# First loads in the order of use and the first projection in halves of its rows, in a two-layer transformer trunk on one core

## The chip, the core and the metric

The kernel runs on one core of a Trainium2 chip. TensorE (PE in the rows, PEld for its weight loads) multiplies, VectorE (DVE) and ScalarE (ACT) do the elementwise work, GpSimd (POOL) makes constants, SyncE (SP) issues the transfers between HBM and the core's memory; 16 DMA engines carry them. The metric is the device time of one execution in microseconds (us). Three runs of the kernel before gave 1373.3 to 1374.16 us, median 1373.78 us.

## The reference, cut to what matters

Two layers, 256 rows of x, width 1024. Each layer begins with one wide projection of x, and this first projection of the first layer is where the change lies:

```python
def hybrid_mixer(x, cos, sin, w_in, ...):
    proj = x @ w_in                                   # (256, 1024) @ (1024, 6664)
    u, qkv_dil, qkv_fox, f_logit, g_logit = jnp.split(proj, offsets, axis=-1)
    y_ssm = s5_mixer(u, ...)
    qd, kd, vd = ...                                  # from qkv_dil
    qd = partial_rotary(qd, cos, sin) * scale         # cos, sin from positions
    qf, kf, vf = ...                                  # from qkv_fox
    ...
```

Then come the three mixer branches, cross-attention into a memory, and a feed-forward part (dense in layer 0, eight experts in layer 1), each followed by a layer norm.

## The kernel before

Every f32 product is made of three passes of TensorE: the high parts of both factors, then high by low, then low by high (`mm3`). The weights come in pieces of 1 MB (`raw`), taken from a list, `plan`, in the order in which they are used. `split` cuts half a piece (128 x 1024) into its parts: ScalarE copies the high part, VectorE subtracts it for the low part. x must lie with its features along the partitions: `half_features` transposes four 128 x 128 blocks on TensorE, and `parts` writes the high part (`xth`, ScalarE) and the low part (`xtl`, VectorE). `x_features(0)` does that for rows 0 to 127, `x_features(1)` for rows 128 to 255.

`load_x` issues the first loads: two halves of the rows 0 to 127, the first piece of weights, two halves of the rows 128 to 255, the second piece. The first projection makes `vv` (256 x 512) from these two pieces in `gemm_xs`. Its argument `mid` is x's second half: the products of the first 128 rows are made with both pieces (24 products of 128 x 512 columns), then `mid` is called, then the 24 products of the other 128 rows follow; those with their splits are kept in `held`.

Beside this, generators (`side`) hand out small work, one piece at each `tick`: the constants (`make_constants`, at its end `rope_tables`, which loads the positions and makes the sines of the rotary embedding) and the parameters of the state space branch (`ssm_params`). The order of the instructions on each engine is made by a scheduler when the program is built, from the order of the code and its own durations; each engine then works in that order, and an instruction that waits holds all that stand behind it on that engine. `issue_after` binds an instruction in that order behind another. Loads are issued by SyncE's queue; eight semaphores take turns, so a load waits for the landing of the eighth before it.

Of the kernel before, what the change touches and what calls it, by code (L numbers as in the profile page):

```python
# [1 line left out]

# [5 lines left out]
F32 = mybir.dt.float32  # L8
F32R = mybir.dt.float32r
I32 = mybir.dt.int32  # L10
# [6 lines left out]
P = 128  # L17
D = 1024
KT = 8
S = 256  # L20
NT = 2
# [27 lines left out]
HALVES = (slice(0, 512), slice(512, 1024))  # L49


class Trunk:
# [5 lines left out]
    def __init__(self, tc, a, out):  # L58
        self.tc, self.nc, self.a, self.out = tc, tc.nc, a, out
        self.depth = 2  # L60
        self.on_pool = 0
        self.plan, self.issued, self.pos, self.raw = [], 0, 0, {}
        self.sides, self.later = [], []

# [148 lines left out]
    def split(self, raw, keep=False):  # L215

        k, n = raw.shape[1], raw.shape[2]
        if keep:
            t = self.slot([P, 2, k, n], F32R, name="split")
        else:  # L220
            t = self.splits.tile([P, 2, k, n], F32R, name="split", tag="split")
        self.nc.scalar.copy(t[:, 0], raw)  # L222
        if self.on_pool > 0:

            self.on_pool -= 1
            for i in range(2):
                self.nc.gpsimd.tensor_sub(t[:, 1, i], raw[:, i], t[:, 0, i].bitcast(F32))
        else:
            self.nc.vector.tensor_sub(t[:, 1], raw, t[:, 0].bitcast(F32))  # L229
        return t[:, 0], t[:, 1]  # L230

    def parts(self, dst, ps, scale=1.0):

        self.nc.scalar.mul(dst[0], ps, scale)  # L234
        hi = dst[0].bitcast(F32)
        if scale == 1.0:
            self.nc.vector.tensor_sub(dst[1], ps, hi)  # L237
        else:
            self.nc.vector.scalar_tensor_tensor(dst[1], ps, scale, hi, op0=ALU.mult, op1=ALU.subtract)

    def mm3(self, ps, left, right, first, last):
        (lh, ll), (rh, rl) = left, right
        mm = self.nc.tensor.matmul
        mm(ps, lh, rh, start=first, stop=False)  # L244
        mm(ps, lh, rl, start=False, stop=False)  # L245
        mm(ps, ll, rh, start=False, stop=last)  # L246

    def gemm_ws(self, chunks, k, mov, evac):

# [18 lines left out]
                        pair += 1  # L268
                self.tick()

    def gemm_xs(self, groups, stat, evac, mid=None, kt=KT):

        for g in range(groups):
            ps, held = None, []
            for half in range(kt // 4):
                raw = self.next_raw()
                n = raw.shape[2]
                if ps is None:  # L280
                    ps = [self.bank(self.mm)[:, :n] for _ in range(NT)]

                def one(t, k, parts):
                    for j in range(2):
                        s = slice(t * P, t * P + P)
                        self.mm3(ps[t], (stat[0][:, k + j, s], stat[1][:, k + j, s]),
                                 (parts[0][:, j], parts[1][:, j]), k + j == 0, k + j == kt - 1)

                for c in range(0, 4, 2):
                    parts = self.split(raw[:, c:c + 2])  # L290
                    k = half * 4 + c
                    if mid:
                        held.append((k, parts))
                        one(0, k, parts)
                    else:
                        for t in range(NT):
                            one(t, k, parts)
                        self.tick()
            evac(g, 0, ps[0])
            if mid:  # L300
                mid()
            for k, parts in held:
                one(1, k, parts)
                self.tick()
            evac(g, 1, ps[1])

    def banks4(self, name):
# [127 lines left out]
    def rope_tables(self):  # L435
        import numpy as np

        nc, c = self.nc, self.const
        pos = c.tile([P, NT], I32, name="pos")
        nc.sync.dma_start(pos, self.a["positions"].rearrange("o (t p) -> p (o t)", p=P),  # L440
                          allow_slow_non_contiguous=True)
        posf = c.tile([P, NT], F32, name="posf")
        nc.vector.tensor_copy(posf, pos)
        inv = np.float32(ROPE_THETA) ** (-np.arange(0, 16, 2, dtype=np.float32) / np.float32(16))
        freq = c.tile([P, ROPE_HALF], F32, name="freq")
        for j in range(ROPE_HALF):
            nc.gpsimd.memset(freq[:, j:j + 1], float(inv[j]))
        ang = c.tile([P, NT, ROPE_HALF], F32, name="ang")
        for t in range(NT):
            nc.vector.tensor_scalar_mul(ang[:, t], freq, posf[:, t:t + 1])  # L450
        self.rcos = c.tile([P, NT, ROPE_HALF], F32, name="rcos")
        self.rsin = c.tile([P, NT, ROPE_HALF], F32, name="rsin")
        w = c.tile([P, NT, ROPE_HALF], F32, name="rw")
        self.sincos(ang, self.rsin, self.rcos, w)
        nc.vector.tensor_scalar_add(self.rcos, self.rcos, 1.0)
# [21 lines left out]
        return (self.slot([P, KT, S], F32R, name=name + "h"), self.slot([P, KT, S], F32R, name=name + "l"))  # L477

    def load_x(self):
        self.x = self.slot([P, NT, D], name="x")  # L480
        src = self.a["x"].rearrange("o (t p) d -> p (o t) d", p=P)
        for t in range(NT):
            for h in range(2):
                s = slice(h * 512, h * 512 + 512)
                self.nc.sync.dma_start(self.x[:, t, s], src[:, t, s])
            self.prefetch(t + 1)

    def load_gb(self, g, b):
        gb = self.slot([P, 2, D], name="gb")
# [41 lines left out]
    def ssm_params(self):  # L531

        nc, c, a = self.nc, self.const, self.a
        n = DEPTH * NPIECE
        rows = self.work([n, 3, P], "lamrows")
        nc.sync.dma_start(rows[:, 0], a["ssm_lambda_re"].rearrange("l (i g) s -> (l i) (g s)", g=2))
        nc.sync.dma_start(rows[:, 1], a["ssm_lambda_im"].rearrange("l (i g) s -> (l i) (g s)", g=2))
        ldt = self.sm([n, 2], "ldt", bufs=1)
        nc.sync.dma_start(ldt, a["ssm_log_dt"].rearrange("l (i g) -> (l i) g", g=2))
        drow = self.work([DEPTH * 4, P], "drow")  # L540
        nc.sync.dma_start(drow, a["ssm_d"].rearrange("l (k p) -> (l k) p", p=P))
        nc.vector.tensor_copy(rows[:, 2].rearrange("p (g s) -> p g s", g=2),
                              ldt[:, :, None].to_broadcast([n, 2, 64]))
        yield
        ps = self.bank(self.aux, "lam")
        for j in range(3):
            nc.tensor.transpose(ps[:, j * n:(j + 1) * n], rows[:, j], self.ident[:n, :n])
        nc.tensor.transpose(ps[:, 3 * n:3 * n + 8], drow, self.ident[:8, :8])
        lam = self.work([P, 16, n], "lamw")
        nc.vector.tensor_copy(lam[:, 0:3].rearrange("p a b -> p (a b)"), ps[:, :3 * n])  # L550
        self.dskip = c.tile([P, DEPTH * 4], F32, name="dskip")
# [1 line left out]
        lre, lim, dt, are, ang, sn, cm, w, th, e1, e2, den, t1, t2, nr, ni = (lam[:, j] for j in range(16))  # L553
# [412 lines left out]
    def mixer(self, l):  # L966
        nc = self.nc

        def ssm_all():
            if l == 0:  # L970
                yield from self.ssm_params()
                yield from self.ssm_layer_params(0)
            yield from self.ssm_steps(l)
# [2 lines left out]
        vv = self.slot([P, 2, NT, BW], name="vv")  # L976
        if l == 0:
            ssm = self.side(ssm_all(), .4)
        self.gemm_xs(1, self.xt, lambda g, t, ps: nc.scalar.copy(vv[:, 0, t], ps),
                     mid=lambda: self.x_features(1))  # L980
        if l == 0:
            self.load_mem()
            for t in range(NT):
# [59 lines left out]
        w, gp = self.gelu, self.gelup  # L1043
# [18 lines left out]
        ps = self.gemm_down(KT, lambda k, t: tuple(m[:, k, t * P:t * P + P] for m in mp))  # L1062
# [396 lines left out]
```

## Time and profile before

| | |
|---|---|
| median of three runs | 1373.78 us |
| the profiled execution | 1373.86 us |
| its span, first to last instruction | 1372.1 us |
| TensorE busy in the span | 1342.3 us, 98% |
| VectorE busy | 1075.0 us, 78% |
| ScalarE busy | 814.4 us, 59% |
| last product of the first projection starts | 23.99 us |

TensorE is busy nearly throughout, so a time is lost or won where it stands idle or runs slowly. The list of instructions in order of time gives each one's start, duration, engine, line of the kernel, operation and operands, and in brackets how long the engine stood idle before it and for whom. A busy TensorE is modelled: the distance from one product's start to the next is the better measure of its pace.

### The profile page before, as it was taken

What the parts mean: (1) busy time and instruction counts of PE and PEld (TensorE: products, weight loads), DVE (VectorE), ACT (ScalarE), POOL (GpSimd) and SP (SyncE); (2) the same over time, 40 slices, a digit from 0 to 9 for tenths busy, and PEclk for the clock granted to TensorE, in tenths of its full rate; (3) what the DMA queues carried; (4) which work ended last, traced back from release to release, by engine and by line L of the source; (5) the groups of instructions that cost most, each with busy time, mean ns of one, the idle gap of its engine ahead of it and who ended that gap; (6) DMA issues with size and microseconds to landing.
All of it is one profiled execution on the core that took longest, in us unless ns stands there. A gap on an engine that the chain in (4) does not pass through costs nothing. (4 is left out here: it accounts for less than half of the span.)

```text
span 1372.1 us, 20754 instructions
## 1 busy us (share of the span) xinstructions
PE 1342.3 (98%) x8086; PEld 1163.5 (85%) x8086; DVE 1075.0 (78%) x1721; ACT 814.4 (59%) x1186; POOL 39.1 (3%) x65
## 2 busy tenths in 40 slices
PE   7999999999999999999999999998999999999995
PEld 6997778889899999889777888987888888888884
DVE  6898779687675696567779668758989889888987
ACT  5658654554454644444766454543877777877873
POOL 1000000000000000010000000014000000000000
PEclk9999999999999999999999999997999999999998
DMA  9452457744672347634235764462999999999980
GB/s 308 125 185 71 145 185 254 268 142 165 214 232 92 123 138 253 224 111 151 93 123 199 274 227 133 171 255 74 354 357 323 355 343 330 359 337 335 345 321 32
DMA packets 175114, 299.37 MB, mean 218 GB/s; under 512 B 19288, under 2 KB 88992, under 8 KB 175008
## 3 DMA queue, kind: packets, MB, share of 16 engines
q1 hardware_dynamic: 175008, 297.97, 62.7%
q8 instruction: 65, 1.06, 0.3%
q14 instruction: 41, 0.34, 0.1%
HBM read 295.85 MB, written 1.05 MB: 216 GB/s over the span
## 5 line engine op out<-in xcount | busy, mean ns | idle before, releaser
L229 DVE TENSOR_TENSOR split<-raw,split 128x1024 fp32r<-128x1024 f32 (+1 forms) x555 | 648.5, 1191 | 196.0 <-ACT split L222 189.7
L222 ACT CAST split<-raw 128x1024 fp32r<-128x1024 f32 (+1 forms) x558 | 564.1, 1027 | 319.3 <-PE bank L246 121.1
L244 PE MATMUL bank<-xth,split 128*128 128x256 f32 x672 | 191.2, 285 | 0.0
L245 PE MATMUL bank<-xtl,split 128*128 128x256 f32 x672 | 190.3, 283 | 0.0
L246 PE MATMUL bank<-xth,split 128*128 128x256 f32 x672 | 190.2, 283 | 0.0
L244 PE MATMUL gu<-split,xgh 128*128 128x512 f32 (+1 forms) x384 | 144.4, 376 | 0.0
L245 PE MATMUL gu<-split,xgh 128*128 128x512 f32 (+1 forms) x384 | 143.0, 372 | 0.1
L246 PE MATMUL gu<-split,xgl 128*128 128x512 f32 (+1 forms) x384 | 142.7, 372 | 0.0
L244 PE MATMUL bank<-split,xth 128*128 128x512 f32 x320 | 130.0, 406 | 4.6 <-ACT xth L234 4.6
L244 PEld LDWEIGHTS bank<-xth,split 128*128 128x128 f32 x672 | 128.9, 192 | 0.6 <-issue 0.2
L245 PEld LDWEIGHTS bank<-xtl,split 128*128 128x128 f32 x672 | 128.9, 192 | 0.4
L246 PEld LDWEIGHTS bank<-xth,split 128*128 128x128 f32 x672 | 128.9, 192 | 0.1
L246 PE MATMUL bank<-split,xtl 128*128 128x512 f32 x320 | 125.8, 394 | 0.3 <-DVE xtl L237 0.3
L245 PE MATMUL bank<-split,xth 128*128 128x512 f32 x320 | 125.7, 393 | 0.0
L245 PEld LDWEIGHTS gu<-split,xgh 128*128 128x128 f32 x384 | 72.2, 188 | 11.3 <-DVE split L229 1.4
L246 PEld LDWEIGHTS gu<-split,xgl 128*128 128x128 f32 x384 | 72.1, 188 | 10.2
L244 PEld LDWEIGHTS gu<-split,xgh 128*128 128x128 f32 x384 | 72.2, 188 | 10.0
L244 PEld LDWEIGHTS bank<-split,xth 128*128 128x128 f32 x320 | 60.5, 189 | 19.8 <-ACT xth L234 5.5
L246 PEld LDWEIGHTS bank<-split,xtl 128*128 128x128 f32 x320 | 60.5, 189 | 14.3 <-DVE xtl L237 0.9
L245 PEld LDWEIGHTS bank<-split,xth 128*128 128x128 f32 x320 | 60.7, 190 | 11.3 <-DVE split L229 0.2
L245 PE MATMUL yd<-split,hth 128*128 128x512 f32 x176 | 69.1, 393 | 0.0
L246 PE MATMUL yd<-split,htl 128*128 128x512 f32 x176 | 68.8, 391 | 0.0
(420 smaller groups left out, 2336.1 us busy)
## 6 DMA issues: line engine op xcount, KB each, us to landing
raw<-in_w_in_dram SPq DMA_DIRECT2D x52, 1024.0 KB, 5.3
raw<-in_moe_w_down_dram SPq DMA_DIRECT2D x40, 1024.0 KB, 6.7
raw<-in_moe_w_gate_dram SPq DMA_DIRECT2D x32, 1024.0 KB, 7.4
raw<-in_moe_w_up_dram SPq DMA_DIRECT2D x32, 1024.0 KB, 7.3
raw<-in_w_branch_dram SPq DMA_DIRECT2D x12, 1024.0 KB, 5.0
raw<-in_moe_w_gate_dram SPq DMA_DIRECT2D x16, 768.0 KB, 7.1
raw<-in_moe_w_up_dram SPq DMA_DIRECT2D x16, 768.0 KB, 6.5
raw<-in_ffn_w_gate_dram SPq DMA_DIRECT2D x11, 1024.0 KB, 5.3
```

The source lines that it names most:

```text
L222: self.nc.scalar.copy(t[:, 0], raw)
L229: self.nc.vector.tensor_sub(t[:, 1], raw, t[:, 0].bitcast(F32))
L244: mm(ps, lh, rh, start=first, stop=False)
L245: mm(ps, lh, rl, start=False, stop=False)
L246: mm(ps, ll, rh, start=False, stop=last)
```

## The change

The loads: `load_x` issues the first piece of weights in two transfers of half its size, and the positions, which `rope_tables` loaded late, directly behind x's second half and ahead of the second piece of weights. The positions are 256 single numbers of 4 bytes, one for each row of x, put on 128 partitions.

The order: `queued` binds the splits of the first projection on ScalarE behind x's features. The first projection runs in halves of its rows only over the first piece: 12 products of the rows 0 to 127, `mid`, 12 products of the rows 128 to 255, and then the second piece for all rows (`late=False`). The eight transposes of `mid` are bound behind the product before them. In `ssm_params` two `yield` are added, and a copy and the transposes are bound behind a split and a product.

```diff
@@ split, queued, parts, mm3
-        self.nc.scalar.copy(t[:, 0], raw)
+        with self.queued():
+            self.nc.scalar.copy(t[:, 0], raw)
...
-            self.nc.vector.tensor_sub(t[:, 1], raw, t[:, 0].bitcast(F32))
+            self.rest = self.nc.vector.tensor_sub(t[:, 1], raw, t[:, 0].bitcast(F32))
...
+    @contextlib.contextmanager
+    def queued(self):
+        with contextlib.ExitStack() as stack:
+            for i in self.ahead:
+                stack.enter_context(self.tc.issue_after(i.ins))
+            yield
...
-        self.nc.scalar.mul(dst[0], ps, scale)
+        self.featured = self.nc.scalar.mul(dst[0], ps, scale)
...
-        mm(ps, ll, rh, start=False, stop=last)
+        self.product = mm(ps, ll, rh, start=False, stop=last)
@@ gemm_xs
+                def second():
+                    with self.tc.issue_after(self.product.ins):
+                        mid()
+                    if self.ahead:
+                        self.ahead = [self.featured]
+                    for k, parts in held:
+                        one(1, k, parts)
+                        self.tick()
+
                 for c in range(0, 4, 2):
                     parts = self.split(raw[:, c:c + 2])
                     k = half * 4 + c
-                    if mid:
+                    if mid and (late or half == 0):
                         held.append((k, parts))
                         one(0, k, parts)
                     else:
                         for t in range(NT):
                             one(t, k, parts)
                         self.tick()
+                if mid and not late and half == 0:
+                    second()
             evac(g, 0, ps[0])
-            if mid:
-                mid()
-            for k, parts in held:
-                one(1, k, parts)
-                self.tick()
+            if mid and late:
+                second()
             evac(g, 1, ps[1])
@@ rope_tables
-        pos = c.tile([P, NT], I32, name="pos")
-        nc.sync.dma_start(pos, self.a["positions"].rearrange("o (t p) -> p (o t)", p=P),
-                          allow_slow_non_contiguous=True)
         posf = c.tile([P, NT], F32, name="posf")
-        nc.vector.tensor_copy(posf, pos)
+        nc.vector.tensor_copy(posf, self.positions)
@@ load_x
         for t in range(NT):
-            for h in range(2):
-                s = slice(h * 512, h * 512 + 512)
+            for s in HALVES:
                 self.nc.sync.dma_start(self.x[:, t, s], src[:, t, s])
-            self.prefetch(t + 1)
+            if t == 0:
+                w, k, n = self.plan[0]
+                self.raw[0] = raw = self.slot([P, k, n], name="raw")
+                for j in range(0, k, 2):
+                    self.nc.sync.dma_start(raw[:, j:j + 2], w[:, j:j + 2])
+                self.issued = 1
+        self.positions = self.const.tile([P, NT], I32, name="pos")
+        self.nc.sync.dma_start(self.positions, self.a["positions"].rearrange("o (t p) -> p (o t)", p=P),
+                               allow_slow_non_contiguous=True)
+        self.prefetch(2)
@@ ssm_params
+        yield
+        yield
+        with self.tc.issue_after(self.rest.ins):
+            nc.vector.tensor_copy(rows[:, 2].rearrange("p (g s) -> p g s", g=2), ...)
         yield
         ps = self.bank(self.aux, "lam")
+        with self.tc.issue_after(self.product.ins):
...
@@ mixer
+        if l == 0:
+            self.ahead = [self.featured]
         self.gemm_xs(1, self.xt, lambda g, t, ps: nc.scalar.copy(vv[:, 0, t], ps),
-                     mid=lambda: self.x_features(1))
+                     mid=lambda: self.x_features(1), late=l > 0)
+        self.ahead = []
```

SyncE's queue at the start of the program, before (behind the first two loads of x). `raw` is a piece of weights, `pos` the positions, `lamrows`, `ldt` and `drow` are parameters of the state space branch:

```order
L202 DMA raw<-in_w_in_dram 128x4x512
L485 DMA x<-in_x_dram 128x512 x2
L202 DMA raw<-in_w_in_dram 128x4x512
L390 DMA bforget<-in_b_forget_dram 128x16
L536 DMA lamrows<-in_ssm_lambda_re_dram 32x128
L202 DMA raw<-in_w_in_dram 128x8x256 x2
L537 DMA lamrows<-in_ssm_lambda_im_dram 32x128
L539 DMA ldt<-in_ssm_log_dt_dram 32x2
L541 DMA drow<-in_ssm_d_dram 8x128
L1069 DMA mem<-in_mem_dram 128x2x1024
L202 DMA raw<-in_w_xk_dram 128x8x256
L440 DMA pos<-in_positions_dram 128x2x1
```

The same queue at the same place, now:

```order
L506 DMA raw<-in_w_in_dram 128x2x512 x2
L501 DMA x<-in_x_dram 128x512 x2
L509 DMA pos<-in_positions_dram 128x2x1
L204 DMA raw<-in_w_in_dram 128x4x512
L409 DMA bforget<-in_b_forget_dram 128x16
```

The positions moved from behind the fifth whole piece of weights to the seventh load of the program.

VectorE from the last of the first small constants on, before. `split<-raw,split` is the low part of half a piece of weights, `xtl` the low part of x's features:

```order
L384 CAST fmask<-fi 128x8
L229 TENSOR_TENSOR split<-raw,split 128x1024
L237 TENSOR_TENSOR xtl<-tp,xth 128x4x128
L229 TENSOR_TENSOR split<-raw,split 128x1024
L237 TENSOR_TENSOR xtl<-tp,xth 128x4x128
L229 TENSOR_TENSOR split<-raw,split 128x1024 x2
```

The same engine from the last of its first small constants on, now. `posf` to `ang` are the angles of the rotary embedding:

```order
L418 TENSOR_SCALAR gmask<-gmask 128x2
L459 CAST posf<-pos 128x2
L466 TENSOR_SCALAR ang<-freq,posf 128x8 x2
L445 TENSOR_SCALAR rw<-ang 128x16
L446 TENSOR_SCALAR rw<-rw 128x16
L448 SCALAR_TENSOR_TENSOR ang<-rw,ang 128x16 x3
L248 TENSOR_TENSOR xtl<-tp,xth 128x4x128 x2
L367 CAST distf<-dist 128x384
L232 TENSOR_TENSOR split<-raw,split 128x1024 x2
```

The cast of the positions and seven instructions behind it now stand ahead of x's first low parts and of the first split. Before, that cast was the 38th instruction behind the cast into `fmask`; now it is the sixth.

## Rows read from the trace of the kernel before

**Rows 1.** The page, busy time of TensorE and its share of the span.

```profile
PE 1342.3 (98%) x8086; PEld 1163.5 (85%) x8086; DVE 1075.0 (78%) x1721; ACT 814.4 (59%) x1186; POOL 39.1 (3%) x65
```

**Rows 2.** Busy time by stretch: bounds, length, engines (instructions), granted clock, DMA share, GB/s.

```profile
10.31:14.48 4.17, 4.17 (x11) 3.28 (x12) 3.67 (x5) 3.09 (x4) 0.00 (x0) 1.00 1.06 356
14.48:24.21 9.73, 9.73 (x46) 7.96 (x45) 7.91 (x21) 5.14 (x7) 0.00 (x0) 1.00 0.98 313
24.21:640.00 615.79, 612.48 (x4234) 546.20 (x4233) 463.56 (x863) 325.25 (x508) 11.01 (x16) 1.00 0.53 175
936.00:954.00 18.00, 17.04 (x70) 15.46 (x71) 13.19 (x45) 4.63 (x8) 8.62 (x7) 0.53 0.15 45
1362.50:1372.10 9.60, 0.00 (x0) 0.00 (x0) 6.42 (x14) 0.00 (x0) 1.47 (x2) 0.51 0.30 111
```

**Rows 3.** Instructions in order of time, TensorE, the first projection (start, duration).

```profile
4.94 1.11 PE L468 MATMUL tp<-ident,x 128*128 128x128 f32 x4 [0.20 <-DMA x<-in_x_dram]
10.31 0.80 PE L244 MATMUL bank<-split,xth 128*128 128x512 f32 x1 [4.26 <-ACT xth L234]
...
11.19 0.78 PE L245 MATMUL bank<-split,xth 128*128 128x512 f32 x1
...
13.25 0.63 PE L246 MATMUL bank<-split,xtl 128*128 128x512 f32 x1
13.68 0.63 PE L244 MATMUL bank<-split,xth 128*128 128x512 f32 x1
...
14.48 0.39 PE L246 MATMUL bank<-split,xtl 128*128 128x512 f32 x1
14.71 0.40 PE L244 MATMUL bank<-split,xth 128*128 128x512 f32 x1
...
15.64 0.60 PE L468 MATMUL tp<-ident,x 128*128 128x128 f32 x4
...
24.21 0.28 PE L244 MATMUL bank<-xth,split 128*128 128x256 f32 x1
```

**Rows 4.** Instructions in order of time, SyncE's queue, loads issued.

```profile
2.19 0.98 SPq L485 DMA_DIRECT2D x<-in_x_dram  x2
3.21 0.54 SPq L202 DMA_DIRECT2D raw<-in_w_in_dram  x1
3.79 1.03 SPq L390 DMA_DIRECT2D bforget<-in_b_forget_dram  x1
...
15.27 0.46 SPq L202 DMA_DIRECT2D raw<-in_w_xk_dram  x1
15.77 2.76 SPq L440 DMA_DIRECT2D pos<-in_positions_dram  x1
```

**Rows 5.** DMA issues, narrow stretches round these loads: size, us from issue to landing.

```profile
x<-in_x_dram SPq DMA_DIRECT2D x2, 256.0 KB, 7.2
...
raw<-in_w_in_dram SPq DMA_DIRECT2D x1, 1024.0 KB, 9.5
bforget<-in_b_forget_dram SPq DMA_DIRECT2D x1, 8.0 KB, 9.9
...
raw<-in_w_xk_dram SPq DMA_DIRECT2D x1, 1024.0 KB, 10.2
pos<-in_positions_dram SPq DMA_DIRECT2D x1, 1.0 KB, 9.9
```

**Rows 6.** Instructions in order of time, VectorE: a split, x's low part, small ones.

```profile
9.79 1.23 DVE L229 TENSOR_TENSOR split<-raw,split 128x1024 fp32r<-128x1024 f32 x1 [5.43 <-ACT split L222]
...
16.58 0.69 DVE L237 TENSOR_TENSOR xtl<-tp,xth 128x512 fp32r<-128x512 f32 x1 [0.37 <-ACT xth L234]
...
17.58 0.35 DVE L348 CAST distf<-dist 128x384 f32<-128x384 int32 x1
...
53.15 0.17 DVE L819 TENSOR_SCALAR fw<-fw 128x16 f32<-128x16 f32 x1 [0.30 <-ACT fw L818]
53.35 0.17 DVE L821 TENSOR_SCALAR fw<-fw 128x16 f32<-128x16 f32 x1
```

**Rows 7.** Instructions in order of time, ScalarE: the first split.

```profile
8.72 1.04 ACT L222 CAST split<-raw 128x1024 fp32r<-128x1024 f32 x1 [6.64 <-DMA raw<-in_w_in_dram]
```

More of the change, by code (lines that the diff above doesn't have):

```diff
@@ L1 @@
+import contextlib
 import math
@@ L269, in gemm_ws, with gemm_xs @@
                 self.tick()
-    def gemm_xs(self, groups, stat, evac, mid=None, kt=KT):
+    def gemm_xs(self, groups, stat, evac, mid=None, kt=KT, late=True):
         for g in range(groups):
@@ L541, in ssm_params @@
         nc.sync.dma_start(drow, a["ssm_d"].rearrange("l (k p) -> (l k) p", p=P))
-        nc.vector.tensor_copy(rows[:, 2].rearrange("p (g s) -> p g s", g=2),
-                              ldt[:, :, None].to_broadcast([n, 2, 64]))
+        yield
+        yield
+        with self.tc.issue_after(self.rest.ins):
+            nc.vector.tensor_copy(rows[:, 2].rearrange("p (g s) -> p g s", g=2),
+                                  ldt[:, :, None].to_broadcast([n, 2, 64]))
         yield
         ps = self.bank(self.aux, "lam")
-        for j in range(3):
-            nc.tensor.transpose(ps[:, j * n:(j + 1) * n], rows[:, j], self.ident[:n, :n])
-        nc.tensor.transpose(ps[:, 3 * n:3 * n + 8], drow, self.ident[:8, :8])
+        with self.tc.issue_after(self.product.ins):
+            for j in range(3):
+                nc.tensor.transpose(ps[:, j * n:(j + 1) * n], rows[:, j], self.ident[:n, :n])
+            nc.tensor.transpose(ps[:, 3 * n:3 * n + 8], drow, self.ident[:8, :8])
         lam = self.work([P, 16, n], "lamw")
@@ L978, in mixer @@
             ssm = self.side(ssm_all(), .4)
+        if l == 0:
+            self.ahead = [self.featured]
         self.gemm_xs(1, self.xt, lambda g, t, ps: nc.scalar.copy(vv[:, 0, t], ps),
-                     mid=lambda: self.x_features(1))
+                     mid=lambda: self.x_features(1), late=l > 0)
+        self.ahead = []
         if l == 0:
```

## The prediction

> **What bounds the kernel now.** First the page: TensorE is busy for 98% of the span [rows 1], so I look for the stretches in which it is not, or is slow. The busy times by stretch show that the change can only matter at the front: from 24.21 to 640 us TensorE works 612.48 of 615.79 us, so all that is to be had there is 3.3 us in seven or so small gaps, and behind that the order of instructions is the same in both kernels [rows 2]. So third, the front in order of time [rows 3]. Three things are to be seen. The first transposes end at about 6.05 us, and the first product starts at 10.31, after 4.26 us of idle time; the second product starts at 11.19. From there products of 512 columns start every 0.43 us (13.25 to 13.68), which is 512 columns at 1.2 GHz; from 14.48 on they start every 0.23 us, which is the level of 2.4 GHz. (The granted clock of that stretch reads 1.00, since nothing is recorded before the rise; the distance between starts is the evidence.) The last product of the first projection is followed at 24.21 by the next one. 24.21 us is the number to beat: what the new front makes of it is, to first order, what the whole kernel gains or loses, because TensorE is nearly full behind it.
>
> Why the first product waits: ScalarE could begin the first split only at 8.72, when the first piece had landed, and copied x's features behind it [rows 7]. This is what the change attacks.
>
> **Part 1, what the new loads give.** The first half of the first piece now lands earlier. The whole piece landed at 8.7 [rows 7]; its second half is 0.5 MB, and the DMA engines move 356 GB/s [rows 2], so the first half should land near 8.7 - 1.5 = 7.2 us (an estimate). x's first features need only x, and are copied by about 6.7. ScalarE's high part takes 1.04 [rows 7], so the first product, which needs high parts only, can start near 8.4 instead of 10.31. That one product gains 1.9 us. The second needs the split's low part, from VectorE.
>
> **Part 2, what VectorE now waits for.** In the new order the cast of the positions stands ahead of x's low parts and of the first split. VectorE works in its order, so all of these wait until the positions have landed. When is that? They are issued behind x's second half, so behind 2 MB in the queue. x's last quarter was issued at about 2.7 and took 7.2 us, so it landed at 9.9 [rows 4, 5]; the same bytes stand ahead of it now. A small load lands behind what was issued before it: the positions themselves landed at 15.77 + 9.9 = 25.7, right behind a piece of weights issued ahead of them (15.27 + 10.2 = 25.5), that is 0.2 behind; `bforget` landed at 13.7, 1.0 behind the second piece (12.7) [rows 4, 5]. So the positions land between 9.9 (with x) and 10.9; I take 10.2, 0.3 behind x, near the row of the positions themselves. Before, nobody waited for them: the first split on VectorE ran at 9.79 [rows 6].
>
> From 10.2 VectorE has this chain. Eight small instructions, seven of them each waiting for the one before at a distance of 0.20 (53.15 to 53.35) and one beside: 1.45 us. Two low parts of x, 0.69 each, which overlap a little: 1.3. The cast `distf`, 0.35, of which 0.3 counts. The split, 1.23, of which 1.2 counts [all rows 6]. Sum: 10.2 + 1.45 + 1.3 + 0.3 + 1.2 = 14.45, and the second product starts 0.15 behind, as before (9.79 + 1.23 to 11.19) [rows 3, 6]: **14.6 us**, where it was 11.19. TensorE stands idle from 9.2 to 14.6. The second split is ready in time: its high part by about 9.8, its low part at 15.7, wanted at about 17.2.
>
> **Part 3, the clock.** Before, 4.2 us passed from the first product to the pace of 2.4 GHz (10.31 to 14.48), and TensorE was busy throughout [rows 2, 3]. I take the same 4.2 us from 14.6, since before it lies 5.4 us of idle time: slow until 18.8. In it 4.2 / 0.43 = 9.8 products are made; with the one at 8.4, eleven of the 48. The twelfth ends the first block at 19.1. No row prices another rise. Each us of slow pace costs 0.47 us (1 - 0.23/0.43); between no slow time and twice as much the term moves by -2.0 to +2.0 us.
>
> **Part 4, the halves of rows.** Now come x's eight other transposes and its features. Before, four transposes began at 15.64 and the low part was done at 16.58 + 0.69 = 17.27, 1.63 later [rows 3, 6]. Two products need no low part of x, the third does; so the 15th product starts at 19.1 + 1.63 = 20.7, and 34 products are left at 0.23: 7.8 us. The second piece landed at 12.7 [rows 4, 5] and is split while the 12 held products run; its two splits (1.04 on ScalarE, 1.2 on VectorE each) are done by about 23.1 and 24.3, wanted at 23.4 and 26.2. The front ends at 20.7 + 7.8 = **28.5 us, 4.3 later** than 24.21.
>
> **What is moved besides.** The positions' 256 small packets delay the second piece, which has 8 us to spare in the new order. SyncE's loads of `wfew` and `brt` now stand ahead of `mem`; `mem` is wanted only when the work behind the front is under way. ScalarE gets two more table loads, one in the front behind the second split, where it waits for TensorE anyway, one later, where ScalarE is busy 325 of 616 us [rows 2]. The state space parameters come later on all engines; TensorE's small gaps can shrink or grow for that. I take nothing, with -1.2 to +2.0 as bounds (about a third of the 3.3 us closed, or some two thirds as much again opened). The low clock near 936 us and near 1363 us [rows 2]: at the second TensorE has no work at all, so nothing is lost there; the first costs some 8 us either way, and I take it to move along with the program.
>
> **Sum.** The profiled execution took 1373.86 us, 1372.1 of it span, 1.8 around it; the median is 1373.78, so the two agree. 1373.8 + 4.3 = **1378.1 us**, slower by 0.31%. About 0.2% (2.75 us) is what a measurement of this kernel can tell from no change.
>
> **Rivals.** *The positions do not hold VectorE* (the other side: not slower). Mechanism: the positions land ahead of x's second half, at best by 5.2 us, so that the small instructions and x's low parts (1.45 + 1.3 + 0.3) are done when the first high part is, at 7.2 + 1.04 = 8.2. Then the first split is done at 9.5, the second product starts at 9.7, the clock rises at 13.9, the first block ends at 14.0, and 14.0 + 1.63 + 7.8 = 23.4: 0.8 us gained, 1373.0. So even unhindered the change brings little: what the earlier start gives, the uncovered features of x's second half take back. Each us later than 5.2 costs one: with a landing at 6.0 the time is that of before, and up to 8.7 it stays within 0.2%. Against it: in both pairs of rows the small load lands behind the larger one issued before it [rows 4, 5]. The Trainium skill (DMA: Bandwidth & Descriptors, section on queues, rings and completion order) speaks for it: loads of one issuing engine need not complete in the order of issue. By that rule alone the time would be this rival's 1373.0. The traces so far bear it out in no pair that I read, hence its small chance.
>
> *Held, but paid back.* The clock is up sooner (the work from 8.4 counts, or the slow time is shorter), or small gaps behind close: with 2.0 us off the clock term and some of the 1.2 us off the gaps the loss is 1 to 2.5 us, 1375.5. For it: only one rise is in the trace. Against: the long idle time ahead of 14.6.
>
> *More than that.* The clock rises 2 us later than I take, and the moved state space work opens new waits of 2 us or more: 1381.5 and above. For it: TensorE waits in its order, and a good part of that order behind the front was rearranged.
>
> *The low clock near 936 us falls on other work, or does not come.* It covers 18 us at 0.53 [rows 2], so its loss could go or double: 8 us either way. Three runs within 0.9 us speak against its moving freely.
>
> **How the numbers follow.** Forecast (2.75 to 7.5 us slower) 0.74; positions not holding 0.10; paid back 0.09; more than that 0.05; low clock 0.02, half on each side. Slower by over 0.2%: 0.74 + 0.05 + 0.01 = 0.80. Within 0.2%: 0.10 + 0.09, less 0.02 in which these end beyond a gain of 2.75 us: 0.17. Faster: 0.03. For the range, the landing moves the sum by -0.3 to +0.7, the clock by -2.0 to +2.0, the gaps by -1.2 to +2.0; as they hardly fall together, 1375.4 to 1381.2 holds the forecast's middle and most of the paid back case.
>
> **What would show it.** In the profile of the changed kernel: VectorE idle until about 10.2 ahead of the cast of the positions, put down to a DMA; the first split on VectorE ending near 14.4; TensorE idle some 5 us between its first and second product; the pace of 0.23 us from about 18.8; the product of 256 columns that follows the projection at 28.5. I am wrong if the cast runs at 8.7 us or earlier, if products run at 0.23 us soon after 14.6, or if TensorE's gaps from the front to 640 us sum to much else than 3.3 us.

## The result, and the profile after

The changed kernel took 1382.94 us (median of 4 runs, 1382.49 to 1383.6), the kernel before 1373.54 us beside it (4 runs, 1372.6 to 1374.16): 1.0071 times as long, with a 95% interval from 1.0059 to 1.0084 (the two medians alone give 1.0068). It is 9.4 us slower; 4.3 were forecast, and 1382.94 lies above the range. The sign and the mechanism at the front were right, its size was not, and more than a third of the loss lies at places that the forecast took to cost nothing.

The profiled execution of the changed kernel took 1383.6 us, 1381.9 of it span. First, VectorE at the front, in order of time (start, duration, engine, line, operation; in brackets the idle time before it and what ended it). It answers to [rows 6]:

```profile
10.40 0.17 DVE L459 CAST posf<-pos 128x2 f32<-128x2 int32 x1 [5.70 <-DMA pos<-in_positions_dram]
...
13.47 2.35 DVE L232 TENSOR_TENSOR split<-raw,split 128x1024 fp32r<-128x1024 f32 x2
```

VectorE stands idle for 5.70 us until the positions are there, and only then comes what the first projection waits for. TensorE in the first projection of the changed kernel, which answers to [rows 3]:

```profile
8.56 0.80 PE L255 MATMUL bank<-split,xth 128*128 128x512 f32 x1 [2.95 <-ACT split L225]
14.75 0.80 PE L256 MATMUL bank<-split,xth 128*128 128x512 f32 x1 [5.39 <-DVE split L232]
...
19.18 0.63 PE L257 MATMUL bank<-split,xtl 128*128 128x512 f32 x1
19.60 1.71 PE L484 MATMUL tp<-ident,x 128*128 128x128 f32 x8
21.35 0.51 PE L255 MATMUL bank<-split,xth 128*128 128x512 f32 x1
...
22.07 0.50 PE L257 MATMUL bank<-split,xtl 128*128 128x512 f32 x1
...
29.91 0.28 PE L255 MATMUL bank<-xth,split 128*128 128x256 f32 x1
```

The whole first block of twelve products and nearly all of the eight transposes behind it ran at the slow pace; the trace records the full clock at 20.98 us, and the first product at the fast pace is that at 21.35. The last row stood at 24.21 before: the front ends 5.70 us late.

The second place is far behind the front, in layer 1's first projection. TensorE there, first in the kernel before, then in the changed one:

```profile
597.80 0.39 PE L244 MATMUL bank<-split,xth 128*128 128x512 f32 x1
598.45 1.32 PE L468 MATMUL tp<-ident,x 128*128 128x128 f32 x8 [0.25 <-DVE x L517]
```

```profile
604.63 0.39 PE L255 MATMUL bank<-split,xth 128*128 128x512 f32 x1
607.07 0.50 PE L256 MATMUL bank<-split,xth 128*128 128x512 f32 x1 [2.05 <-DVE split L232]
...
608.54 1.91 PE L484 MATMUL tp<-ident,x 128*128 128x128 f32 x8
```

And VectorE at that place in the changed kernel, the end of the layer norm and the split that TensorE waits for:

```profile
604.48 1.41 DVE L542 SCALAR_TENSOR_TENSOR x<-x,lnrs,gb 128x512 f32<-128x512 f32 x2
605.80 1.22 DVE L232 TENSOR_TENSOR split<-raw,split 128x1024 fp32r<-128x1024 f32 x1
```

Before, the eight transposes of x filled the time in which VectorE, busy with the layer norm, had not yet made the next split's low part. Now they stand behind the products, TensorE waits 2.05 us, and then its clock falls. Busy time of the changed kernel by stretch shows that (bounds, length, busy time and instructions of TensorE, its weight loads, VectorE, ScalarE and GpSimd, granted clock, DMA share, GB/s):

```profile
29.91:605.10 575.19, 571.82 (x3934) 508.27 (x3932) 432.80 (x802) 304.95 (x478) 8.70 (x15) 1.00 0.51 172
605.10:608.50 3.40, 1.43 (x5) 1.08 (x6) 1.92 (x3) 0.00 (x0) 0.00 (x0) 0.94 0.00 0
608.50:612.00 3.50, 3.50 (x14) 2.90 (x13) 1.38 (x2) 1.78 (x3) 0.00 (x0) 0.57 0.00 0
...
946.50:963.50 17.00, 16.56 (x66) 14.99 (x67) 12.23 (x43) 4.62 (x8) 8.09 (x6) 0.51 0.14 46
```

The third row is the fall: granted clock 0.57, that is 1.2 GHz for most of 3.5 us. The last row is the low clock that stood near 936 us before [rows 2]; it has moved along.

Where the 9.7 us between the two spans arise is seen if the start of each TensorE product is compared with that of the same product, by its number, in the kernel before (both have 8086 instructions there). This table is worked out from the traces, each time counted from the start of its span; it has all profiled kernels of this study, whose edits follow (in the last three the added products are left out of the count, and the full clock is there before the second product). "Slow" is the time from the second product (in the kernel before and its variants from the first, since there the two stand together) to the moment at which the trace records the full clock.

| Offset against before, us, at the product that before starts at | 24.21 | 83.61 | 318.87 | 668.40 | 1134.22 | 1358.32 | slow, us |
|---|---|---|---|---|---|---|---|
| changed kernel | 5.70 | 5.29 | 6.83 | 9.92 | 9.95 | 9.94 | 6.2 |
| positions first | -0.05 | -0.47 | 1.08 | 4.74 | 4.08 | 4.08 | 4.7 |
| layer 1 free | 3.70 | 3.28 | 4.81 | 4.85 | 3.86 | 3.86 | 3.0 |
| before, layer 1 bound | 0.40 | 0.43 | 0.52 | 3.63 | 2.18 | 2.18 | 3.9 |
| positions first, layer 1 free | -0.46 | -0.88 | 0.67 | 0.71 | -0.24 | -0.24 | 3.5 |
| no yields | 5.65 | 4.89 | 4.92 | 7.13 | 6.46 | 6.43 | 5.2 |
| all three taken out | 0.86 | 1.59 | 1.41 | 1.39 | 1.28 | 1.30 | 5.4 |
| the same, second profile | -0.50 | -1.26 | -1.38 | -1.38 | -1.67 | -1.65 | 2.4 |
| before, positions early | 0.56 | 0.99 | 1.07 | 1.08 | 0.51 | 0.50 | 3.4 |
| ten products added | -1.63 | -2.39 | -2.61 | -2.59 | -2.61 | -2.62 | |
| the same, second profile | -1.49 | -0.16 | -0.32 | -0.28 | -0.80 | -0.79 | |
| nineteen products added | -1.67 | -1.92 | -1.53 | -1.49 | -2.09 | -2.09 | |

The changed kernel loses 5.7 us in the front, 1.5 between 84 and 319 us, 3.1 between 319 and 668 us (the place shown), and nothing behind. The second loss has its waits in the list of TensorE's waits from 56 to 300 us of the changed kernel (who waited for what: us in total, times, longest):

```profile
PE py L931 <- ACT pts L924: 0.7, 1, 0.7
PE bank L256 <- DVE split L232: 0.7, 1, 0.7
PE fcum L863 <- DVE lf L859: 0.6, 1, 0.6
PE bank L255 <- DVE merged L981: 0.4, 1, 0.4
```

### The profile page after: what moved, and what is told of

The parts are those of the page before. It is cut to its first block, busy times and chain, and to the rows that moved or that the text cites. A ratio compares the mean times of both kernels' runs of the same rounds, so it can differ in the third digit from the quotient of the medians.

```text
span 1381.9 us, 20753 instructions
## 1 busy us (share of the span) xinstructions
PE 1346.3 (97%) x8086; PEld 1166.2 (84%) x8086; DVE 1074.8 (78%) x1721; ACT 817.7 (59%) x1188; POOL 38.9 (3%) x65
```

## Experiments

My theory at this point: three parts of the change cost time, each by itself. The positions ahead of the first splits on VectorE (front); the binding of x's transposes to the product before them, which also acts in layer 1; and the two added `yield`s in the state space parameters (84 to 319 us). The rivals were that one of them causes another's loss further on, or that the early load, not its place on VectorE, does the harm. The first four kernels ran on one chip beside 25 runs of the kernel before (median 1373.3 us), the next four beside 27 (1373.08), the last three beside 27 (1373.27).

**Positions first.** The changed kernel with the load of the positions moved ahead of x.

```diff
     def load_x(self):
+        self.positions = self.const.tile([P, NT], I32, name="pos")
+        self.nc.sync.dma_start(self.positions, self.a["positions"].rearrange("o (t p) -> p (o t)", p=P), ...)
...
-        self.positions = self.const.tile([P, NT], I32, name="pos")
-        self.nc.sync.dma_start(self.positions, self.a["positions"].rearrange("o (t p) -> p (o t)", p=P), ...)
```

> The changed kernel with one edit: the positions are the first load of the program. The order of TensorE and ScalarE is that of the changed kernel; on VectorE the cast of the positions stands ahead of the small constants. Theory (VectorE is held by the landing of the positions at 10.3 us): the first split on VectorE ends near 9.6 instead of 14.7, the second product starts near 9.8 instead of 14.75, the first product of 256 columns near 24 to 25.5 instead of 29.9, and the time falls by 4.5 to 6 us to about 1377 to 1378.5. Rival (the front is slow for the transposes in one block, the late clock and the table load): the front stays within 1.5 us of 29.9 and the time above 1381.5.

Measured: 1377.34 us (9 runs), 1.0028 of before [1.0018, 1.0039]. VectorE and then TensorE at its front:

```profile
2.94 0.96 DVE L459 CAST posf<-pos 128x2 f32<-128x2 int32 x1 [2.94 <-DMA pos<-in_positions_dram]
```

```profile
8.24 0.79 PE L255 MATMUL bank<-split,xth 128*128 128x512 f32 x1 [1.62 <-ACT split L225]
9.54 0.80 PE L256 MATMUL bank<-split,xth 128*128 128x512 f32 x1 [0.50 <-DVE split L232]
```

With nothing ahead of them in the queue the positions are there at 2.94 instead of 10.40, the hole of 5.39 us between the first two products shrinks to 0.50, and the front's 5.7 us are gone (offset -0.05). What is left, 1.5 and 3.7 us further on, is untouched; at layer 1's place it is more than the 3.1 us of the changed kernel, since there the clock fell as soon as the hole ended (recorded at 601.30 us, the product behind the hole starts at 601.34).

**Layer 1 free.** The changed kernel, with the binding in layer 0 only (`late` is set in layer 1).

```diff
-                    with self.tc.issue_after(self.product.ins):
+                    with contextlib.ExitStack() as stack:
+                        if not late:
+                            stack.enter_context(self.tc.issue_after(self.product.ins))
                         mid()
```

> The changed kernel with one edit: the eight transposes of x's second half are bound behind the product before them in layer 0 alone, so that in layer 1 they stand in front of the products that wait for a split, as before. Theory (the binding opened a wait of 2.05 us at 605 us in layer 1, and the clock fell behind it for 3.4 us): no such wait, no fall of the clock at 608 us, time lower by 3.1 us, about 1379.8. Rival (the clock falls there for another reason, as a clock that falls at a set time): the fall stays and no more than 1.5 us is won.

Measured: 1378.21 us (5 runs), 1.0038 [1.0024, 1.0053]. TensorE at the place:

```profile
602.62 0.39 PE L255 MATMUL bank<-split,xth 128*128 128x512 f32 x1
603.26 1.32 PE L486 MATMUL tp<-ident,x 128*128 128x128 f32 x8 [0.25 <-DVE x L544]
```

The transposes stand where they stood before, there is no hole and no fall of the clock, and the offset does not grow between 319 and 668 us (4.81 to 4.85). It came out 1.6 us below what was expected: in its profile the slow pace lasted 3.0 us only, and about 1 us came back where the clock is low near 936 us.

**Before, layer 1 bound.** The opposite: the kernel before with the binding added in layer 1 alone (by then `self.ssm` is filled).

```diff
-        mm(ps, ll, rh, start=False, stop=last)
+        self.product = mm(ps, ll, rh, start=False, stop=last)
...
             if mid:
-                mid()
+                if len(self.ssm) > 0:
+                    with self.tc.issue_after(self.product.ins):
+                        mid()
+                else:
+                    mid()
```

> The kernel before with one edit: in layer 1 the eight transposes of x's second half are bound behind the product before them. Theory: slower by 3.1 us, about 1376.7, with the wait of 2 us at about 598 us and the fall of the clock behind it. Rival (the fall of the clock needs the shifted time of the changed kernel): slower by 1.5 us or less and no fall.

Measured: 1376.24 us (10 runs), 1.0024 [1.0015, 1.0034]. TensorE, and the stretch of the fall:

```profile
600.78 0.50 PE L245 MATMUL bank<-split,xth 128*128 128x512 f32 x1 [2.08 <-DVE split L229]
...
602.23 1.91 PE L472 MATMUL tp<-ident,x 128*128 128x128 f32 x8
```

```profile
601.80:605.20 3.40, 3.40 (x13) 2.70 (x12) 1.09 (x2) 1.78 (x3) 0.00 (x0) 0.51 0.00 0
```

The hole (2.08 us), the fall of the clock and 3.1 us of offset (0.52 to 3.63) appear in a kernel whose front was not touched. So this loss does not come from the late front; the binding makes it. 1.45 us of it come back near 936 us, where the stretch of low clock is shorter this time.

**Positions first, layer 1 free.** Both edits together.

> The changed kernel with both edits, positions loaded first and layer 1 free. Theory (the terms add): 4.5 to 6 and 3.1 off, 1374 to 1375.5; what is left over the kernel before is the 1.3 us between 60 and 250 us and up to 1 us of the front. Rival (something else in the new front costs): above 1377.

Measured: 1374.64 us (10 runs), 1.0009 [0.9999, 1.0018]. This is as expected. What is left is the step between 84 and 319 us (-0.88 to 0.67).

**No yields.** The changed kernel without the two added yields, all else kept.

```diff
-        yield
-        yield
         with self.tc.issue_after(self.rest.ins):
```

> The changed kernel without the two added yields in the state-space parameters' generator; positions, halves and the binding to the first projection's products stay, in both layers. Theory (the two yields push the state-space work later among layer 0's products, and TensorE loses 1.35 us there between 60 and 250 us of the changed kernel's profile): the front still ends some 5.7 us late and layer 1's place still costs 3.1 us, but the 1.35 us are gone, so about 1381.6 us. Rival (the 1.35 us are a later consequence of the late front, whatever the order): the offset between 60 and 250 us stays near 1.3 us and the time is that of the changed kernel, 1382.9 us.

Measured: 1380.65 us (4 runs), 1.0056 [1.0041, 1.0071], 2.3 us below the changed kernel. TensorE's waits from 56 to 300 us:

```profile
PE pt L920 <- DVE ssmw L768: 0.9, 1, 0.9
PE fcum L861 <- DVE lf L857: 0.7, 1, 0.7
PE py L929 <- ACT pts L922: 0.3, 1, 0.3
```

The waits for a split and for `merged` are gone, and the offset stands still from 84 to 319 us (4.89 to 4.92). So the two yields made that step: it is 1.5 to 1.6 us in the four profiles that have them, and between -0.2 and 0.0 in the three of the changed kernel without them and without added products. The waits in the two lists, 2.4 and 1.9 us in sum, differ by less than the 1.5 us; what the rest is, the lists don't tell, and it stays open. At layer 1's place this run shows something else, on TensorE:

```profile
605.16 0.50 PE L256 MATMUL bank<-split,xth 128*128 128x512 f32 x1 [2.09 <-DVE split L232]
...
606.43 1.04 PE L484 MATMUL tp<-ident,x 128*128 128x128 f32 x8
```

The hole is the same, but the clock did not fall (the transposes took 1.04, not 1.91), and the place cost 2.2 us instead of 3.1. So of the 3.1 us some 2.2 are the hole, and 0.9 the clock (1.5 in the run with the positions first), which fell behind the hole in three of the four profiles that have it and in no profile without it.

**All three taken out.** Positions first, layer 1 free, no yields.

> The changed kernel with the positions as its first load, the binding in layer 0 only, and without the two added yields. Theory (these three are all that the change costs, and the front without the hold ends 0.5 to 0.9 us early): 1.0 to 1.5 us less than the version that keeps the yields (1374.6 us), so 1373.0 to 1373.6 us, at or slightly below the kernel before. Rival (the yields cost nothing by themselves): 1374.6 us again.

Measured: 1371.86 us (11 runs), 0.9991 [0.9981, 1.0000]. A second time, on another chip:

> The version with the three costs taken out, once more beside the two with added products, on one chip. Theory (its front differs from run to run by how long the clock stays at its lower level, everything behind the front stands still): 1371.9 us again within 0.6 us, and in the profile an offset against the kernel before that is set by 60 us and changes by less than 0.3 us from there to the end. Rival (some of what it gains or loses lies behind the front): the offset moves by more than that behind 60 us.

Measured: 1372.46 us (11 runs), 0.9995 [0.9986, 1.0004]. The changed kernel's loss is gone whole, 10.5 to 11.1 us, and both medians lie below the 1373.0 to 1373.6 us that were expected at first. The two profiled runs, 1374.98 and 1371.85 us, are of one and the same program. TensorE's second product and the product that follows the first projection, in the first profile and in the second:

```profile
10.07 0.80 PE L256 MATMUL bank<-split,xth 128*128 128x512 f32 x1 [0.46 <-DVE split L232]
...
25.07 0.28 PE L255 MATMUL bank<-xth,split 128*128 128x256 f32 x1
```

```profile
10.10 0.79 PE L256 MATMUL bank<-split,xth 128*128 128x512 f32 x1 [0.47 <-DVE split L232]
...
23.71 0.28 PE L255 MATMUL bank<-xth,split 128*128 128x256 f32 x1
```

The second products agree, the ends of the front differ by 1.36 us: the full clock came at 15.51 in the one and at 12.52 in the other, and 3.0 us at 0.47 are 1.4. That is half of what parts them: at the product of 83.61 they are 2.85 us apart. In the first profile one small instruction of VectorE took 2.37 us, while GpSimd (POOL) worked, and TensorE then waited 1.24 us for the low part of the memory's features; in the second the same instruction took 0.19, and TensorE did not wait for that part at all. First profile, then second:

```profile
36.75 2.68 POOL L819 TENSOR_TENSOR wfewp<-wfew,wfewp 128x1024 fp32r<-128x1024 f32 x1 [32.41 <-ACT wfewp L818]
37.12 2.37 DVE L615 TENSOR_TENSOR lamw<-lamw 128x32 f32<-128x32 f32 x1
...
40.35 0.39 PE L256 MATMUL bank<-mtl,split 128*128 128x256 f32 x1 [1.24 <-DVE mtl L248]
```

```profile
35.76 0.19 DVE L615 TENSOR_TENSOR lamw<-lamw 128x32 f32<-128x32 f32 x1
```

So the theory of the second run, by which only the clock parts the runs, holds for one half of the difference. Behind 84 us both offsets change by 0.3 to 0.4 us in all, a little more than the 0.3 expected; most of what changes in the second lies near 936 us.

**Before, positions early.** The kernel before, with its positions loaded behind x's second half and ahead of the second piece of weights; on VectorE their cast stays behind the first splits.

```diff
-        pos = c.tile([P, NT], I32, name="pos")
-        nc.sync.dma_start(pos, ...)
...
+            if t == 1:
+                self.positions = self.const.tile([P, NT], I32, name="pos")
+                self.nc.sync.dma_start(self.positions, self.a["positions"].rearrange("o (t p) -> p (o t)", p=P), ...)
             self.prefetch(t + 1)
```

> The kernel before with one edit: the positions are loaded early, behind x's second half and ahead of the second piece of the first weights. Their conversion stays behind the first splits in VectorE's order. Theory (the hold comes from the conversion's place ahead of the first split on VectorE, not from the early load itself): no wait of VectorE for the positions ahead of the first splits, the second product within 0.5 us of 14.5 us, and the time within 1 us of the kernel before. Rival (the load itself delays x or the weights behind it on their way into the chip): the first splits or the second product come 1 us or more later, and so does the end.

Measured: 1373.07 us (10 runs), 1.0002 [0.9992, 1.0011]; the cast ran at 18.9 us, and VectorE waited for the positions nowhere. The second product started at 11.73 us. The 14.5 us of the expectation were missed, and could not have been met, since before it stood at 11.19; 11.73 is also its place in the run with layer 1 bound, whose front is that of before. The early load by itself costs nothing; what costs is who stands behind its first reader on VectorE.

**Work for TensorE ahead of the first projection.** If the slow pace is worth up to 2 us, could added work bring the clock up sooner? All three taken out, and ten products of the identity with itself between x's first transposes and the first product.

```diff
+    def warm(self, n):
+        ps = self.bank(self.aux, "warm")
+        for i in range(n):
+            self.nc.tensor.matmul(ps[:, :P], self.ident, self.ident, start=True, stop=True)
...
         self.x_features(0)
+        if l == 0:
+            self.warm(10)
```

> The same as the version with the three costs taken out, and ten 128x128 products of the identity with itself between x's first transposes and the first projection product, in time in which TensorE waits for the first split; their bank is read by nobody, so this adds work and leaves nothing out. Theory (what keeps the clock at its lower level after the second product is that TensorE hardly worked before it, so work ahead of it lets the clock rise earlier; each microsecond less at the lower level is worth about half a microsecond): the fast pace begins 1 to 4 us earlier and the front ends 0.5 to 2 us earlier, 1371.5 to 1373 us. Rival (the idle 1 to 2 us between the first and second product undo it): the fast pace begins where it did, and the time is within 0.3 us of the other version.

> The version with ten products of the identity ahead of the first projection, once more: its runs lay between 1370.4 and 1374.5 us, and the one that was profiled, at 1370.92 us, had the clock up at 8.42 us. Theory (the clock comes up during the added products in some runs and falls back or comes up later in others): a second profile shows the clock up at another time, and the time of that run goes with it at about half a microsecond for each microsecond of lower clock. Rival (the spread has its origin behind the front): the clock is up near 8.4 us again and the offset against the kernel before moves behind 60 us.

Measured: 1372.46 us, 0.9994 [0.9985, 1.0003], and 1371.27 us, 0.9988 [0.9979, 0.9997] (11 runs each). The clock did come up, at 8.32 and 9.62 us, and the front ended at 22.59 and 22.72, some 1.5 us ahead of before. The time shows no gain over the version without the added products that repeats: on the same chip it is 0.6 us longer the first time (1372.46 to 1371.86) and 1.2 us shorter the second (1371.27 to 1372.46). But in the second profile the gain had shrunk to 0.16 us at the product of 83.61. That was not the clock, as I had expected, but a wait of TensorE for the low part of the memory's features, and ahead of it one small instruction on VectorE:

```profile
38.59 0.39 PE L256 MATMUL bank<-mtl,split 128*128 128x256 f32 x1 [1.83 <-DVE mtl L248]
```

```profile
34.97 2.92 POOL L824 TENSOR_TENSOR wfewp<-wfew,wfewp 128x1024 fp32r<-128x1024 f32 x1 [30.62 <-ACT wfewp L823]
35.54 2.40 DVE L642 SCALAR_TENSOR_TENSOR ph<-ph 128x32 f32<-128x32 f32 x1
```

In the first profile the same instruction of VectorE took 0.18, and TensorE had no such wait:

```profile
35.41 0.18 DVE L642 SCALAR_TENSOR_TENSOR ph<-ph 128x32 f32<-128x32 f32 x1
```

So in the second run VectorE's schedule behind the front, and not TensorE's, ended last there. Nineteen products of a zeroed tile, ten of them from the program's start on, came next:

```diff
+            self.zero = self.const.tile([P, P], F32, name="zero")
+            self.nc.vector.memset(self.zero, 0.0)
+            self.warm(10)
             self.load_x()
...
+        if l == 0:
+            self.warm(9)
```

> The version with the three costs taken out, with nineteen added 128x128 products of a zeroed tile with itself, whose bank is read by nobody: ten from the program's start to x's first transposes, nine between these and the first projection product. Work is added, none is left out. Theory (more work ahead brings the clock up before the first projection in every run): the first projection runs at the fast pace throughout, its first 256-column product near 22.5 us, and the time is 1369 to 1371 us, faster than the kernel before. Rival one (products of zeros don't bring the clock up, or the hole between the first and second product undoes it): within 0.5 us of the version without. Rival two (the added products delay x's transposes): the first product behind 9.5 us and the time above the version without.

Measured: 1371.49 us (11 runs), 0.9996 [0.9987, 1.0005]. The full clock was there at 4.72 us, the front ended at 22.54 as expected, the profiled run took 1371.48, half a microsecond above the range expected. Four of the 11 runs took 1373.7 to 1375.6 us; none of those was profiled, so why they were longer stays open. No version of this study is faster than the kernel before by 0.2%; the best ratio, with added products, is 0.9988. What the halves of the rows or the first piece in two transfers give, each by itself, no run shows.

## Why the prediction was wrong where it was wrong

**Part 1** held. The first split began on ScalarE at 7.46 (a landing at 7.2 was estimated), the first product at 8.56 (8.4).

**Part 2** held, the landing and the chain. The cast ran at 10.40 (10.2), the second product at 14.75 (14.6), with 5.39 us of idle time (some 5). The run with the positions first shows that without this hold the front loses nothing, the run with early positions before shows that it is the order on VectorE and not the load.

**Part 3** was mis-sized. The clock was taken to rise 4.2 us behind the second product; in the profiled run it took 6.2. The first block, to have ended at 19.1, ended at 19.60, of which 0.15 came from the later start. **Part 4** inherits half of it: the eight transposes fell into the slow time and took 1.71 us (1.04 in the second profile of the version with all three taken out, where they did not), so that the 15th product started 2.47 us behind the block instead of 1.63, at 22.07 instead of 20.7. The other half is its own: it took the 1.63 from a row of four transposes, where eight now stand ahead of the next product, and in that second profile, at the full clock, the distance is 2.01 (13.85 to 15.86). The 34 products left took 7.84 (7.8). Together the front ended 1.4 us later than the 28.5 that were forecast. The bounds of the clock term (2.0 us either way) held this; the single row of before could not show how far the time moves from run to run, between 2.4 and 6.2 us in the profiles here. With the same hold the front ended 3.70 and 5.65 us late in two other profiles (layer 1 free, no yields), so the 4.3 of the front lies within what one run or another shows.

**What is moved besides** is the step that failed. It took the gaps behind the front to cost nothing, at most 2.0 us, and what lies there cost 4.6 (0.4 came back ahead of 84 us, where the kernel before waits 0.60 us for the low part of the memory's features and the changed one 0.19). The gaps alone tell less than half of it: by the rows of the changed kernel they sum to 5.3 us from the front to 612 us (3.37 to 605.10 and 1.97 behind), where before they were 3.3, and the forecast had named a sum much other than 3.3 as a sign of being wrong. The rest of the 4.6 is work that ran slowly or at other distances, which a sum of gaps does not hold. Two things were missed. The binding of x's transposes was costed as a part of the front (part 4), though the function that has it is called in layer 1 too; there the transposes had been what TensorE did while a split was late. That is 3.1 us of the loss, with a fall of the clock that none of the forecast's terms contained. The busy times by stretch, from which the forecast read that the change can only matter at the front, show no order; in the two profiles TensorE's order differs at this place as well. And the state space work that comes later was named, but priced at nothing: it cost 1.5 us, by the two yields alone. The statement that TensorE's full stretch from 24.21 to 640 us leaves only 3.3 us to be had was true as a bound on gains, and no bound on losses.

**The low clock near 936 us** moved along with the program in the changed kernel (no change of the offset), as taken. In the other profiles 0.0 to 1.5 us came back between 668 and 1134 us, where it lies.

**The rivals.** That the positions don't hold VectorE was wrong of the order written, and the run with the positions first is that rival made true: it gave the front 0.05 us where 0.8 were worked out, and 0.5, 0.5 and -0.9 us in the three other profiles of the changed front without a hold or added products, as the slow time was short or long. The Trainium skill (DMA: Bandwidth & Descriptors, section on queues, rings and completion order), by which loads of one issuing engine need not complete in order, allowed it; in the three profiles in which the cast waits for them (changed kernel, layer 1 free, no yields) the positions did not overtake the 2 MB ahead of them: they came about 0.2 us behind x's last quarter, 10.40 against 10.15 us in the changed kernel. "More than that" named the right time, 1381.5 and above, and half of the mechanism: a clock that rises 2 us later and new waits of the rearranged work. It had a chance of 0.05, since I asked only whether the state space work would open waits and not what else the diff's new condition binds. The sum closes: 5.7 + 1.5 + 3.1 is 10.3, less 0.4 between 24 and 84 us, is 9.9, the offset at the end.

## What to carry to other kernels

Before a small load is moved forward, look up who reads it first and what stands behind that reader in its engine's order: the early load cost nothing, but its cast, put ahead of the first splits on VectorE, made the first projection wait 5 us for data that nobody needed yet. A condition that is put into a shared function acts at each of its calls, so go through the new order at every call, and ask there what the moved work had been covering. On an engine that is 98% busy the little idle time left limits what can be gained and says nothing on what can be lost.

## What was not expected of the hardware

The time from the second product to the full clock was 2.4 to 6.2 us in the profiles, and 2.4 and 5.4 in two profiles of one program: at 0.47 us for each, 1.4 of the 3.0 us between the ends of these two. A hole of 2.05 to 2.09 us on TensorE in layer 1's first projection was followed by about 3.4 us at half clock in three profiles and not in the fourth. The long instructions of VectorE go with GpSimd: in each of the thirteen profiles one instruction of VectorE was longer than elsewhere while GpSimd worked on `wfewp`. In the nine without the yields it is a small one, 0.17 to 0.19 us elsewhere, that took 1.2 to 2.4 us and ended 0.04 to 0.05 us behind GpSimd's; in the four with the yields it is a split, 2.27 instead of 1.23 us. Which one it is changes from run to run of the same program, and the cost depends on who waits: 1.24 and 1.83 us of TensorE in the two profiles shown, none in three others. No run moves GpSimd's work, so that it holds VectorE is read from these times and not shown by an experiment.
